# Attention q and k projected with the weights stationary and both token tiles as one moving operand, v of groups 0 to 2 first

## The chip, the cores and the metric

The kernel runs on one core of a Trainium2 chip. The metric is the device time of one execution in microseconds (us), as the median of several runs. TensorE (PE) multiplies matrices, VectorE (DVE) and ScalarE (ACT) do elementwise work and move results out of PSUM, GpSimd (POOL) and SyncE (SP) mostly start transfers.

## What is computed

Four layers on 256 tokens of width 1024, in fp32. Each layer is a SwiGLU block, a mixer and another SwiGLU block, each followed by a layer norm. The mixers of the four layers are a state-space mixer, "fox" attention, "moba" attention and the state-space mixer again. The change touches the two attention mixers.

```python
def fox_attention(x, w_in, b_f, w_out):           # 16 heads of 64
    q, k, v, f_logit = split(x @ w_in)            # 1024 + 1024 + 1024 + 16 columns
    cum = cumsum(log_sigmoid(f_logit + b_f))
    logits = q k^T * 64**-0.5 + (cum[q] - cum[k]), causal
    return softmax(logits) v  @ w_out

def moba_attention(x, w_in, w_out):               # one block of 256 keys for 256 tokens, so
    q, k, v = split(x @ w_in)                     # this is plain causal attention
    return softmax(causal(q k^T * 64**-0.5)) v @ w_out
```

## The kernel before

The 256 tokens are two tiles of 128. Each tile is a generator (`stream`, line 793), `sts[0]` and `sts[1]`, called tile 0 and tile 1 below (`t` in the code). The weights come in pieces of at most 128 x 2048 fp32 (1 MB). `load` (line 170) fetches a piece and splits it into `wh` (fp32r, by ACT) and the rest `wl` (by DVE). Activations are split likewise into `xh` and `xl` by `to_T` (line 204), after four PE transposes for each half. A product is three matmuls (`mm3`, line 186): `xh` with `wh`, `xh` with `wl`, `xl` with `wh`. The activations are the stationary operand and the weights move through, 512 columns a matmul in `proj512` and 256 in `proj256`.

The outer loop (lines 855 to 869) advances tile 0 by one piece and then tile 1 by the piece two behind, and lets tile 1 catch up at the end of a sublayer. There are five buffers for split pieces. The program order gives priorities. A planner places each engine's instructions by these priorities and by its own estimate of when operands are ready, so what is traced later may go ahead of what waits. `keep_in_program_order` puts an instruction behind everything traced before it on its engine. `tc.high_priority()` lifts layer norms and `to_T`.

An attention sublayer takes its pieces in the order of `ATT_ORDER` (line 44): V0 Q0 V1 Q1 V2 Q2 V3 Q3 and then the four pieces O of the output projection. There are four groups of four heads. Q of a group is two pieces, 256 columns of q and 256 of k side by side, and V is one piece (in fox V0 is two pieces of 1088 columns with the 16 gate columns). For each tile and group:

- `proj512` on the two Q pieces gives q and k with tokens on partitions, in one PSUM bank (24 matmuls of 512 columns).
- `stage_q` (line 672) copies them to SBUF (ACT, line 674), transposes them on PE in four blocks of 128 x 128 (line 199), and writes q times 0.125 (DVE, line 677) and k (ACT, line 678) with features on partitions.
- `stage_v` (line 722) copies v out of its bank. `stage_f` (line 640, fox, V0) first reads the gate columns of that bank.
- `stage_s` (line 682) makes the scores: the mask (line 690), in fox the bias rows (line 695), then q with k (line 702), for tile 1 in two blocks of 128 keys. The first of these is pinned by `keep_in_program_order`. Then comes the softmax.
- `att` (line 729) transposes the probabilities, multiplies them with v (line 747) and splits the result for `down` (line 248), the output projection.

PSUM has eight banks: `GA(0)` and `GA(1)` take the tags acc0 and acc1 with two banks each, shared with the accumulators of `down`; `T()` and `G()` have two each. `at(i, f, ...)` runs a stage behind piece i of its tile.

Of the kernel before, what the change touches and what calls it, by code (L numbers as in the profile page):

```python
# [7 lines left out]
F32 = mybir.dt.float32  # L8
# [7 lines left out]
D = 1024  # L16
# [22 lines left out]

SSM_ORDER = ["X0", "Z0", "X1", "Z1", "O0", "X2", "Z2", "X3", "O1", "Z3",
             "O2", "O3"]
ATT_ORDER = ["V0", "Q0", "V1", "Q1", "V2", "Q2", "V3", "Q3", "O0", "O1", "O2", "O3"]


def ssm_pieces():
# [30 lines left out]
def build(tc, x, wst, ln_g, ln_b, sm_rows, sm_conv, sm_nw, fx_b, out, plan=None):  # L78
# [26 lines left out]
    def tmp(cols, tag, bufs, dt=F32):  # L105
        return spool.tile([128, cols], dt, name=tag, tag=tag, bufs=bufs)

    ident = cpool.tile([128, 128], F32, name="ident")
    make_identity(nc, ident)
    mhalf = cpool.tile([128, 1], F32, name="mhalf")  # L110
# [91 lines left out]
        return tp  # L202

    def to_T(st, h):
        xh = spool.tile([128, KT, 128], FR, name=f"xh{st.t}", bufs=1)
        xl = spool.tile([128, KT, 128], FR, name=f"xl{st.t}", bufs=1)
        for half in range(2):
            tp = transposes(h[:, half * 512:half * 512 + 512], 4)
            sl = slice(half * 4, half * 4 + 4)
            for ins in split(tp.rearrange("p (a b) -> p a b", a=4), xh[:, sl], xl[:, sl]):  # L210
                if opening:
                    tc.keep_in_program_order(ins)
        st.xh, st.xl = xh, xl
# [51 lines left out]
    def proj256(st, ps, w):  # L265
        wh, wl = w
        for k in range(KT):
            mm3(ps[:, :256], st.xh[:, k], st.xl[:, k], wh[:, k * 256:(k + 1) * 256], wl[:, k * 256:(k + 1) * 256],
                k == 0, k == KT - 1)

    def act_split(src, n):
        tp = transposes(src, n)
# [139 lines left out]
    def ssm(st, j):  # L412
# [86 lines left out]
        def stage_back(g):  # L499
            cv = s.cv[g]  # L500
            h8 = slice(g * 8, g * 8 + 8)
            tp = T()
            for k in range(4):
                nc.tensor.transpose(tp[:, k * 128:(k + 1) * 128], cv[:, k, mine], ident)
            tp8 = tp.rearrange("p (a b) -> p a b", a=8)

            def times(tag, rows, bufs):
                o = tmp(512, tag, bufs)
                nc.vector.tensor_mul(o.rearrange("p (a b) -> p a b", a=8), tp8,
                                     rows[:, h8].unsqueeze(2).to_broadcast([128, 8, 64]))  # L510
                return o
            xds[g] = (times(f"xdt{t}", d.dt, 1 + t), times("xD", s.rows[:, 64:96], 2))
            if t == 0:
                s.xe[g] = times("xe", d.de, 1)
# [107 lines left out]
    def fox_small(j):  # L622
        if j in foxs:
            return foxs[j]
        consts()
        s = St()
        s.rows = tmp(16, "rows", 1)
        nc.sync.dma_start(s.rows, bc(fx_b[j:j + 1, :], 16))
        s.kT, s.v = {}, {}
        foxs[j] = s  # L630
        return s

    def attn(st, kind, j):
# [26 lines left out]
        else:  # L660
            key = ("m", j)
            if key not in foxs:
                consts()
                foxs[key] = St()
                foxs[key].kT, foxs[key].v = {}, {}
            s = foxs[key]
        ahs, ps_, vs, kv = {}, {}, {}, {}
        qT = spool.tile([128, 2, 128], F32, name="qT", tag="xD", bufs=2)

        bank = {}  # L670

        def stage_q(g):
            qk = tmp(512, "t2", 4)
            nc.scalar.activation(qk, bank.pop(g), AF.Copy)
            tp = transposes(qk, 4).rearrange("p (a b) -> p a b", a=4)
            kT = kv[g][:, 0:256].rearrange("p (a b) -> p a b", a=2)
            nc.vector.tensor_scalar_mul(qT, tp[:, 0:2], 0.125)
            nc.scalar.activation(kT, tp[:, 2:4], AF.Copy)
            if t == 0:
                s.kT[g] = kT  # L680

        def stage_s(g):

            kT = kv[g][:, 0:256].rearrange("p (a b) -> p a b", a=2)
            rs = spool.tile([128, 12], F32, name="rs", bufs=4)
            parts = [(kT, 0)] if t == 0 else [(s.kT[g], 0), (kT, 128)]
            nk = 128 * len(parts)
            Sv = [f()[:, :2 * nk].rearrange("p (h k) -> p h k", h=2) for f in (T, G)]
            for b in range(2):
                nc.tensor.matmul(Sv[b][:, :, nk - 128:nk], K["mlo"], rep4(2), start=True, stop=True,  # L690
# [6 lines left out]
                    if b == 0:  # L697
                        tc.keep_in_program_order(ins)
            for i in range(2):
                for kt, off in parts:  # L700
                    for b, half in enumerate(halves):
                        ins = nc.tensor.matmul(Sv[b][:, i, off:off + 128], qT[half, i], kt[half, i], start=False,
                                               stop=True, skip_group_check=True)
                        if (i, off, b) == (0, 0, 0):
                            tc.keep_in_program_order(ins)
# [14 lines left out]
            ps_[g] = pt  # L720

        def stage_v(g):
            kv[g] = tmp(512, "xe" if t == 0 and g % 2 else f"xdt{t}", 1 + t)
            vs[g] = kv[g][:, 256:512]
            nc.scalar.activation(vs[g], bank.pop(("v", g))[:, :256], AF.Copy)
            if t == 0:
                s.v[g] = vs[g]

        def att(g):

# [10 lines left out]
            blocks = [vs[g]] if t == 0 else [s.v[g], vs[g]]  # L741
            for i in range(2):
                for kb, v in enumerate(blocks):
                    for b in range(2):
# [22 lines left out]
            at(where["Q", 0, 1], stage_cum)  # L767
        for g in range(ATT_G):
            q = where["Q", g, 1]
            at(q, stage_q, g)  # L770
            wait = 2 if fox and g == 0 else 0
            at(q + 1 + wait, stage_s, g)
            at(where["V", g, int(fox and g == 0)], stage_v, g)
            at(q + 2 + wait, att, g)
        first_o = where["O", 0, 0]
        for i, (kind, g, n) in enumerate(pieces):
            if kind == "Q" and n == 0:
                ps = bank[g] = GA(0) if i < first_o else G()
            elif kind == "V" and n == 0:
                ps = bank["v", g] = GA(1) if i < first_o else G()  # L780
            w = yield
            if kind == "O":
# [1 line left out]
            elif kind == "V" and fox and g == 0:  # L784
                proj512(st, ps, n, w, 272)
            elif kind == "V":
                proj256(st, ps, w)
            else:
                proj512(st, ps, n, w)
            for f, a in post.get(i, ()):  # L790
                f(*a)

# [129 lines left out]
def pack_att(w_in, w_out):  # L922
    P = []
    dn = rows2(w_out)
    for it in ATT_ORDER:
        g = int(it[1])
        sl = slice(g * 256, g * 256 + 256)
        if it[0] == "Q":
            P += cols512(np.concatenate([w_in[:, 0:D][:, sl], w_in[:, D:2 * D][:, sl]], axis=1))
        elif it == "V0" and w_in.shape[1] > 3 * D:  # L930
            P += cols512(np.concatenate([w_in[:, 2 * D:3 * D][:, sl], w_in[:, 3 * D:]], axis=1))
        elif it[0] == "V":
# [60 lines left out]
```

## Time and profile before

| | |
|---|---|
| median of 3 runs | 2125.59 us (2124.63 to 2127.35) |
| the profiled execution | 2124.81 us, of it 2122.9 us span |
| PE / DVE / ACT / POOL busy | 99% / 69% / 55% / 23% of the span |
| granted TensorE clock, mean | 0.999 |
| fox attention | about 757 to 879 us |
| moba attention | about 1248 to 1372 us |

In the timelines a row is: start, duration, engine, line, operation, output and operands, shapes, count, and in brackets an idle time ahead of it and what ended it. Matmul durations include a modelled pipeline end, so two neighbours overlap; what a matmul costs in a stream is the distance between starts. "ga", "gu", "acc" and "tp" are PSUM banks, "t" the copy of q and k that `stage_q` transposes, "xe" and "xdt" the buffers of k and v.

### The profile page before, as it was taken

The numbers are of one execution on the slowest core, as the hardware profiler recorded it, in microseconds if no ns is written. First come the engines' busy times: TensorE is split into PE (matmuls) and PEld (weight loads), VectorE is DVE, ScalarE is ACT, GpSimd is POOL, SyncE is SP. The second block draws the span as 40 slices with busy tenths as digits, with TensorE's granted clock in tenths as the row PEclk, the third lists the DMA queues.
The fourth block names the chain that finished last, engine by engine and source line by source line (L and its number), as shares of the span: only waits on it lengthen the run. The fifth ranks groups of instructions, "written<-read, shape, count | busy, mean of one in ns | idle before, by whom it ended". The sixth has DMA issues, their size and how long they took to land.

```text
span 2122.9 us, 29645 instructions
## 1 busy us (share of the span) xinstructions
PE 2099.0 (99%) x10218; PEld 1735.6 (82%) x10218; DVE 1461.4 (69%) x2829; ACT 1177.0 (55%) x2453; POOL 480.9 (23%) x871
## 2 busy tenths in 40 slices
PE   8999999999999999999999999999999999999998
PEld 7888878888888888788888888788888888788886
DVE  6557888855765585766675575765575578888565
ACT  5545997544544455544444455544445449975442
POOL 2331000233143210043233300034223310002331
PEclk9999999999999999999999999999999999999999
DMA  9665654666576653476566653376666656446662
GB/s 316 224 229 203 215 171 172 217 232 224 189 256 227 224 201 122 165 235 230 204 245 230 222 193 139 123 247 238 225 221 232 221 205 220 173 161 221 230 227 95
DMA packets 227559, 441.72 MB, mean 208 GB/s; under 512 B 20752, under 2 KB 21072, under 8 KB 227408
## 3 DMA queue, kind: packets, MB, share of 16 engines
q1 hardware_dynamic: 198768, 397.73, 52.5%
q0 software_dynamic: 28640, 42.09, 6.8%
q8 instruction: 80, 1.31, 0.3%
q14 instruction: 71, 0.58, 0.1%
HBM read 417.61 MB, written 22.13 MB: 207 GB/s over the span
## 4 chain that ended last, share of the span: by engine, by line
PE 91%; DVE 4%; ACT 2%; DMA 1%; issue 1%; POOL 0%; SPq 0%; DVEq 0%; ACTq 0%
PE gu L187 16%; PE gu L190 16%; PE gu L191 16%; PE acc L191 9%; PE acc L187 9%; PE acc L190 9%; PE ga L187 3%; PE ga L190 3%; PE ga L191 3%; PE tp L199 3%; DVE wl L160 2%; PE gu L550 1%; DMA raw<-in_w_dram 1%; PE gu L747 1%; DVE cv L461 1%
## 5 line engine op out<-in xcount | busy, mean ns | idle before, releaser
L160 DVE TENSOR_TENSOR wl<-raw,wh 128x512 fp32r<-128x512 f32 (+1 forms) x1412 | 889.1, 680 | 363.1 <-ACT wh L159 361.7
L159 ACT ACTIVATE wh<-raw 128x512 fp32r<-128x512 f32 (+1 forms) x1412 | 778.8, 620 | 511.2 <-PE gu L191 230.0
L187 PE MATMUL gu<-wh,xh 128*128 128x512 f32 (+1 forms) x1600 | 619.4, 387 | 2.7 <-ACT wh L159 1.2
L190 PE MATMUL gu<-wl,xh 128*128 128x512 f32 (+1 forms) x1600 | 618.6, 387 | 0.0
L191 PE MATMUL gu<-wh,xl 128*128 128x512 f32 (+1 forms) x1600 | 618.1, 386 | 0.0
L291 POOL DMA_DIRECT2D aT<-turn x640 | 348.3, 551 | 488.4 <-issue 314.7
L187 PEld LDWEIGHTS gu<-wh,xh 128*128 128x128 f32 x1600 | 301.1, 188 | 65.0 <-ACT wh L159 2.0
L187 PE MATMUL acc<-wh,ah 128*128 128x512 f32 x896 | 352.7, 394 | 0.0
L191 PE MATMUL acc<-wh,al 128*128 128x512 f32 x896 | 351.9, 393 | 0.3 <-DVE al L160 0.3
L190 PE MATMUL acc<-wl,ah 128*128 128x512 f32 x896 | 351.5, 392 | 0.0
L190 PEld LDWEIGHTS gu<-wl,xh 128*128 128x128 f32 x1600 | 301.2, 188 | 60.5 <-DVE wl L160 1.0
L191 PEld LDWEIGHTS gu<-wh,xl 128*128 128x128 f32 x1600 | 301.2, 188 | 59.8 <-DVE xl L160 0.4
L315 ACT ACTIVATE t<-gu 128x256 f32<-128x256 f32 x176 | 67.5, 383 | 267.8 <-PE gu L191 247.2
L317 DVE TENSOR_TENSOR t<-t,gu 128x256 f32<-128x256 f32 x176 | 73.4, 417 | 189.6 <-ACT t L315 189.6
L191 PEld LDWEIGHTS acc<-wh,al 128*128 128x128 f32 x896 | 168.3, 188 | 36.5 <-DVE al L160 2.1
L187 PEld LDWEIGHTS acc<-wh,ah 128*128 128x128 f32 x896 | 168.3, 188 | 35.8 <-issue 1.3
L190 PEld LDWEIGHTS acc<-wl,ah 128*128 128x128 f32 x896 | 168.3, 188 | 34.5 <-issue 1.3
L287 POOL DMA_DIRECT2D turn<-tb x160 | 90.4, 565 | 330.9 <-DVE tb L285 298.5
L187 PE MATMUL ga<-wh,xh 128*128 128x512 f32 (+4 forms) x448 | 159.5, 357 | 0.4 <-ACT xh L159 0.4
L190 PE MATMUL ga<-wl,xh 128*128 128x512 f32 (+4 forms) x448 | 156.8, 351 | 0.0
L191 PE MATMUL ga<-wh,xl 128*128 128x512 f32 (+4 forms) x448 | 155.7, 349 | 0.0
L235 POOL TENSOR_TENSOR rstd<-ve,mhalf 128x1 f32<-128x1 f32 x24 | 22.7, 945 | 441.9 <-DVE ve L233 441.9
(181 smaller groups left out, 1655.5 us busy)
## 6 DMA issues: line engine op xcount, KB each, us to landing
raw<-in_w_dram SPq DMA_DIRECT2D x354, 1024.0 KB, 5.3
turn<-tb POOLq DMA_DIRECT2D x160, 128.0 KB, 3.1
aT<-turn POOLq DMA_DIRECT2D x640, 32.0 KB, 3.9
mt<-cums SPq DMA_DIRECT2D x32, 256.0 KB, 4.2
gb<-in_ln_g_dram SPq DMA_DIRECT2D x12, 512.0 KB, 4.7
gb<-in_ln_b_dram SPq DMA_DIRECT2D x12, 512.0 KB, 5.8
nw<-in_sm_nw_dram SPq DMA_DIRECT2D x8, 256.0 KB, 5.4
h<-in_x_dram SPq DMA_DIRECT2D x4, 256.0 KB, 4.9
```

Of the source, the lines that this page charges most:

```text
L159: a = nc.scalar.activation(wh, raw, AF.Copy)
L160: return a, nc.vector.tensor_sub(wl, raw, wh.bitcast(F32))
L187: first = nc.tensor.matmul(o, xh, wh, start=start, stop=False)
L190: nc.tensor.matmul(o, xh, wl, start=False, stop=False)
L191: nc.tensor.matmul(o, xl, wh, start=False, stop=stop)
L199: ins = nc.tensor.transpose(tp[:, j * 128:(j + 1) * 128], src[:, j * 128:(j + 1) * 128], ident)
L235: nc.gpsimd.tensor_tensor(rstd, ve, mhalf, op=ALU.pow)
L287: nc.gpsimd.dma_start(dr, b.rearrange("p q k t -> p (q k t)"))
L291: nc.gpsimd.dma_start(aT[32 * q:32 * q + 32].rearrange("p i k t -> p i (k t)"), dv[q])
L315: nc.scalar.activation(sg, gu[:, :256], AF.Silu)
L317: nc.vector.tensor_mul(a, sg, gu[:, 256:])
L461: nc.vector.scalar_tensor_tensor(cv[:, i], xb[:, i, k:k + S], w[:, k:k + 1], cv[:, i], op0=ALU.mult, op1=ALU.add)
```

## The change

The tiles' `xh` and `xl` become slices of one constant tile `x4`, laid out so that for each k-tile the columns are xh of tile 0, xh of tile 1, xl of tile 0, xl of tile 1. A Q piece now holds 256 columns of q or of k alone, over all eight k-tiles. Tile 0 does nothing with it. Tile 1 calls `proj_T`: for each half of 128 features and each k-tile, three matmuls with a 128 x 128 block of weights stationary and 256 columns (both token tiles) moving. The result has features on partitions already; `stage_q` copies it out once for both tiles, q by ACT with the factor, k by DVE, and no longer transposes. Scores of tile 1 take 256 keys in one matmul. V of groups 0 to 2 comes ahead of the first Q and V3 after the last. Buffers of v hold both tiles. The state-space mixer's "xe" buffer goes from one to two.

```diff
-ATT_ORDER = ["V0", "Q0", "V1", "Q1", "V2", "Q2", "V3", "Q3", "O0", "O1", "O2", "O3"]
+ATT_ORDER = ["V0", "V1", "V2", "Q0", "Q1", "Q2", "Q3", "V3", "O0", "O1", "O2", "O3"]
...
+    x4 = cpool.tile([128, KT, 4, 128], FR, name="x4")
...
-        xh = spool.tile([128, KT, 128], FR, name=f"xh{st.t}", bufs=1)
-        xl = spool.tile([128, KT, 128], FR, name=f"xl{st.t}", bufs=1)
+        xh, xl = x4[:, :, st.t], x4[:, :, 2 + st.t]
...
+    def proj_T(ps, w):
+        wh, wl = w
+        for f in range(2):
+            o = ps[:, f * S:f * S + S]
+            for k in range(KT):
+                sl = slice(k * 256 + f * 128, k * 256 + f * 128 + 128)
+                nc.tensor.matmul(o, wh[:, sl], x4[:, k, 0:2], start=k == 0, stop=False, skip_group_check=True)
+                nc.tensor.matmul(o, wh[:, sl], x4[:, k, 2:4], start=False, stop=False, skip_group_check=True)
+                nc.tensor.matmul(o, wl[:, sl], x4[:, k, 0:2], start=False, stop=k == KT - 1, skip_group_check=True)
...
-        def stage_q(g):
-            qk = tmp(512, "t2", 4)
-            nc.scalar.activation(qk, bank.pop(g), AF.Copy)
-            tp = transposes(qk, 4).rearrange("p (a b) -> p a b", a=4)
...
+        def stage_q(g, n):
+            o = tmp(512, "xdt1" if n else "xD", 2).rearrange("p (a b) -> p a b", a=2)
+            ps = bank.pop((g, n)).rearrange("p (a b) -> p a b", a=2)
+            if n:
+                nc.vector.tensor_copy(o, ps)
+                s.kT[g] = o
+            else:
+                nc.scalar.activation(o, ps, AF.Copy, scale=0.125)
+                s.qT[g] = o
...
-                for kt, off in parts:
-                    for b, half in enumerate(halves):
-                        ins = nc.tensor.matmul(Sv[b][:, i, off:off + 128], qT[half, i], kt[half, i], start=False,
...
+                for b, half in enumerate(halves):
+                    ins = nc.tensor.matmul(Sv[b][:, i], q[half, i], k[half, i], start=False, stop=True,
...
             if t == 0:
-                s.v[g] = vs[g]
+                s.v[g] = tmp(512, "xe", 2) if 0 < g < 3 else tmp(512, "xdt0", 1)
+            nc.scalar.activation(s.v[g][:, t * 256:t * 256 + 256], bank.pop(("v", g))[:, :256], AF.Copy)
...
-            at(q, stage_q, g)
-            wait = 2 if fox and g == 0 else 0
-            at(q + 1 + wait, stage_s, g)
+            if t == 1:
+                at(q - 1, stage_q, g, 0)
+                at(q, stage_q, g, 1)
+            at(q + 3 - t, stage_s, g)
             at(where["V", g, int(fox and g == 0)], stage_v, g)
-            at(q + 2 + wait, att, g)
+            at(q + 4 - t, att, g)
...
-            else:
-                proj512(st, ps, n, w)
+            elif t == 1:
+                bank[g, n] = GA(0)
+                proj_T(bank[g, n], w)
...
-            P += cols512(np.concatenate([w_in[:, 0:D][:, sl], w_in[:, D:2 * D][:, sl]], axis=1))
+            P += cols256(w_in[:, 0:D][:, sl]) + cols256(w_in[:, D:2 * D][:, sl])
```

## Rows read from the trace of the kernel before

**Rows 1.** The page: busy time and share of PE; clock in 40 slices.

```profile
PE 2099.0 (99%) x10218; PEld 1735.6 (82%) x10218; DVE 1461.4 (69%) x2829; ACT 1177.0 (55%) x2453; POOL 480.9 (23%) x871
...
PEclk9999999999999999999999999999999999999999
```

**Rows 2.** Busy time of each engine, clock and DMA, in fox and moba.

```profile
755.00:870.00 115.00, 114.15 (x744) 92.97 (x743) 76.78 (x168) 64.62 (x170) 7.37 (x13) 1.00 0.44 157
...
1260.00:1375.00 115.00, 114.74 (x736) 92.28 (x735) 71.98 (x134) 67.32 (x171) 0.92 (x1) 1.00 0.40 147
```

**Rows 3.** Timeline of PE: first and thirteenth of a run of 512-column matmuls.

```profile
741.85 0.39 PE L187 MATMUL gu<-wh,xh 128*128 128x512 f32 x1
...
744.57 0.39 PE L187 MATMUL acc<-wh,ah 128*128 128x512 f32 x1
```

**Rows 4.** Timeline of PE: 24 matmuls of 256 columns, first and what follows.

```profile
769.54 0.28 PE L187 MATMUL ga<-wh,xh 128*128 128x256 f32 x1
...
772.42 0.40 PE L187 MATMUL ga<-wh,xh 128*128 128x512 f32 x1
```

**Rows 5.** Timeline of PE: four transposes of q and k among 512-column matmuls.

```profile
836.20 0.39 PE L187 MATMUL ga<-wh,xh 128*128 128x512 f32 x1
836.43 0.60 PE L199 MATMUL tp<-ident,t 128*128 128x128 f32 x4
836.78 0.48 PE L190 MATMUL ga<-wl,xh 128*128 128x512 f32 x1
837.10 0.39 PE L191 MATMUL ga<-wh,xl 128*128 128x512 f32 x1
```

**Rows 6.** Timeline of PE: the same among 256-column matmuls.

```profile
839.31 0.28 PE L191 MATMUL ga<-wh,xl 128*128 128x256 f32 x1
839.56 0.66 PE L199 MATMUL tp<-ident,t 128*128 128x128 f32 x4
839.97 0.37 PE L187 MATMUL ga<-wh,xh 128*128 128x256 f32 x1
840.18 0.28 PE L190 MATMUL ga<-wl,xh 128*128 128x256 f32 x1
```

**Rows 7.** Timeline of PE: the same right behind scores, and with waits ahead.

```profile
779.01 0.66 PE L199 MATMUL tp<-ident,t 128*128 128x128 f32 x4 [0.17 <-DVE rowsT L373]
...
807.13 0.66 PE L199 MATMUL tp<-ident,t 128*128 128x128 f32 x4
807.54 0.48 PE L187 MATMUL ga<-wh,xh 128*128 128x512 f32 x1
...
811.51 0.66 PE L199 MATMUL tp<-ident,t 128*128 128x128 f32 x4 [0.25 <-ACT t L674]
...
1257.53 0.33 PE L199 MATMUL tp<-ident,t 128*128 128x128 f32 x1 [0.56 <-ACT t L674]
```

**Rows 8.** Timeline of PE: tile 1's scores and what follows; 512-column fp32 matmul.

```profile
842.86 0.27 PE L702 MATMUL tp<-xdt,qT 64*128 64x128 f32 x1
...
843.85 0.50 PE L187 MATMUL acc<-wh,ah 128*128 128x512 f32 x1
...
240.14 1.02 PE L527 MATMUL gu<-xe,t 128*128 128x512 f32 x2
241.00 1.67 PE L550 MATMUL gu<-xdt,mt 128*128 128x64 f32 x14
```

**Rows 9.** Timelines of PE, then of DVE: start of the fox sublayer.

```profile
756.85 0.28 PE L187 MATMUL ga<-wh,xh 128*128 128x272 f32 x1
...
762.60 0.39 PE L187 MATMUL ga<-wh,xh 128*128 128x512 f32 x1
...
764.34 0.39 PE L187 MATMUL ga<-wh,xh 128*128 128x272 f32 x1
...
765.66 0.16 DVE L642 TENSOR_TENSOR sm<-ga,rows 128x16 f32<-128x16 f32 x1
```

**Rows 10.** Groups by line: writes of both token tiles into one shared tile.

```profile
L482 DVE COPY xb<-tp 128x512 f32<-128x512 f32 (+1 forms) x16 | 10.4, 651 | 2.2 <-PE tp L199 2.2
```

More of the change, by code (lines that the diff above doesn't have):

```diff
@@ L513, in stage_back @@
             if t == 0:
-                s.xe[g] = times("xe", d.de, 1)
+                s.xe[g] = times("xe", d.de, 2)
             tp = T()
@@ L628, in fox_small @@
         nc.sync.dma_start(s.rows, bc(fx_b[j:j + 1, :], 16))
-        s.kT, s.v = {}, {}
+        s.qT, s.kT, s.v = {}, {}, {}
         foxs[j] = s
@@ L664, in attn @@
                 foxs[key] = St()
-                foxs[key].kT, foxs[key].v = {}, {}
+                foxs[key].qT, foxs[key].kT, foxs[key].v = {}, {}, {}
             s = foxs[key]
-        ahs, ps_, vs, kv = {}, {}, {}, {}
-        qT = spool.tile([128, 2, 128], F32, name="qT", tag="xD", bufs=2)
-        bank = {}
-        def stage_q(g):
-            qk = tmp(512, "t2", 4)
-            nc.scalar.activation(qk, bank.pop(g), AF.Copy)
-            tp = transposes(qk, 4).rearrange("p (a b) -> p a b", a=4)
[L676 to L680, printed above, removed]
+        ahs, ps_, bank = {}, {}, {}
+        def stage_q(g, n):
[7 more added lines that the diff above has]
+                s.qT[g] = o
         def stage_s(g):
-            kT = kv[g][:, 0:256].rearrange("p (a b) -> p a b", a=2)
+            nk = 128 * (1 + t)
+            q, k = s.qT[g][:, :, t * 128:t * 128 + 128], s.kT[g][:, :, 0:nk]
             rs = spool.tile([128, 12], F32, name="rs", bufs=4)
-            parts = [(kT, 0)] if t == 0 else [(s.kT[g], 0), (kT, 128)]
-            nk = 128 * len(parts)
             Sv = [f()[:, :2 * nk].rearrange("p (h k) -> p h k", h=2) for f in (T, G)]
@@ L699, in stage_s @@
             for i in range(2):
-                for kt, off in parts:
-                    for b, half in enumerate(halves):
-                        ins = nc.tensor.matmul(Sv[b][:, i, off:off + 128], qT[half, i], kt[half, i], start=False,
-                                               stop=True, skip_group_check=True)
-                        if (i, off, b) == (0, 0, 0):
-                            tc.keep_in_program_order(ins)
+                for b, half in enumerate(halves):
+                    ins = nc.tensor.matmul(Sv[b][:, i], q[half, i], k[half, i], start=False, stop=True,
+                                           skip_group_check=True)
+                    if (i, b) == (0, 0):
+                        tc.keep_in_program_order(ins)
             pt = [tmp(512, "mt", 5) for b in range(1 + t)]
@@ L722, in stage_v @@
         def stage_v(g):
-            kv[g] = tmp(512, "xe" if t == 0 and g % 2 else f"xdt{t}", 1 + t)
-            vs[g] = kv[g][:, 256:512]
-            nc.scalar.activation(vs[g], bank.pop(("v", g))[:, :256], AF.Copy)
             if t == 0:
-                s.v[g] = vs[g]
+                s.v[g] = tmp(512, "xe", 2) if 0 < g < 3 else tmp(512, "xdt0", 1)
+            nc.scalar.activation(s.v[g][:, t * 256:t * 256 + 256], bank.pop(("v", g))[:, :256], AF.Copy)
         def att(g):
@@ L740, in att @@
             o = G()
-            blocks = [vs[g]] if t == 0 else [s.v[g], vs[g]]
+            blocks = [s.v[g][:, n * 256:n * 256 + 256] for n in range(1 + t)]
             for i in range(2):
@@ L769, in attn @@
             q = where["Q", g, 1]
-            at(q, stage_q, g)
-            wait = 2 if fox and g == 0 else 0
-            at(q + 1 + wait, stage_s, g)
+            if t == 1:
+                at(q - 1, stage_q, g, 0)
+                at(q, stage_q, g, 1)
+            at(q + 3 - t, stage_s, g)
             at(where["V", g, int(fox and g == 0)], stage_v, g)
-            at(q + 2 + wait, att, g)
+            at(q + 4 - t, att, g)
         first_o = where["O", 0, 0]
         for i, (kind, g, n) in enumerate(pieces):
-            if kind == "Q" and n == 0:
-                ps = bank[g] = GA(0) if i < first_o else G()
-            elif kind == "V" and n == 0:
+            if kind == "V" and n == 0:
                 ps = bank["v", g] = GA(1) if i < first_o else G()
```

## The prediction

> **What bounds the kernel now.** I read the page first. PE is busy for 99% of the span, and the granted clock is at its upper level (2.4 GHz) in every slice [rows 1]. No other engine is near that. A page is an average, so I then looked at the two stretches that the change touches. In 115 us of fox PE is busy for 114.15, in 115 us of moba for 114.74, while DVE and ACT stand at two thirds or less and the DMA engines at 0.40 to 0.44 with about 150 GB/s [rows 2]. So in both places the order of work already fills PE, and the time changes by what PE must issue, not by what DVE, ACT or the transfers must do. PE's busy time has modelled ends, so I cost everything by distances between starts in the timeline.
>
> **What it costs PE to project in 256 columns.** Twelve matmuls of 512 columns take 744.57 - 741.85 = 2.72 us, or 0.2267 us each [rows 3]. Twenty-four of 256 columns take 772.42 - 769.54 = 2.88 us, or 0.1200 us each [rows 4]. Twice 0.1200 is 0.2400, so the same columns cost 13 ns more in two matmuls than in one. Before, q and k take 4 groups x 2 tiles x 24 = 192 matmuls of 512 columns in a layer, 384 in both layers. After, they take 4 groups x 2 pieces x 48 = 384 of 256 columns, 768 in both. 768 x 0.1200 - 384 x 0.2267 = 92.2 - 87.1 = **+5.1 us**, all of it on PE and so on the path. That the weights are now the stationary operand changes nothing I can see: the 256-column matmuls of before [rows 4] also load a 128 x 128 block each, and `x4[:, k, 0:2]` is 256 neighbouring columns, like their slices of `wh`.
>
> The Trainium skill ("TensorE: Matmul & The Clock Gate", section "Back-to-back issue gap") gives a gap of N/2.4 + 2.5 ns at full clock, which makes 109 ns for 256 columns and 216 for 512. By that the second matmul of a pair would cost 2.6 ns and not 13, and the change +1.0 us in place of +5.1, as an estimate. The trace has 120 and 227 ns, so I keep 5.1, and the rule gives the first rival below.
>
> **What it takes from PE.** `stage_q` ran 16 times (4 groups, 2 tiles, 2 layers), with four transposes each. Their price depends on what stands around them, so I looked at all 16.
>
> - Seven lie among 512-column matmuls, as in the first fence of this kind [rows 5]. From 836.20 to 837.10 is 0.90 us, where two matmuls alone take 0.45: 0.45 us each, 3.15 together. The matmul behind the transposes is late as well, which a count of transposes alone would miss.
> - Four lie among 256-column matmuls, as in the second [rows 6]. From 839.31 to 840.18 is 0.87 us, where two matmuls take 0.24: 0.63 us each, 2.5 together.
> - Two come right behind scores, where PE changes its kind of work anyway: 807.54 - 807.13 = 0.41 us each [rows 7], 0.8 together.
> - Three have a wait ahead, of 0.17, 0.25 and 0.56 us [rows 7]. With 0.45, 0.63 and 0.45 for the block itself that is 0.62, 0.88 and 1.01, 2.5 together.
>
> The sum is 3.15 + 2.5 + 0.8 + 2.5 = **-9.0 us**. As bounds, 16 x 0.41 = 6.6 us if every block were as cheap as the cheapest, 16 x 0.63 = 10.1 if as dear as the second kind.
>
> **Scores.** For tile 1 eight pairs of 128 columns become four pairs of 256 (each fp32 matmul has two records, and the two halves of 64 rows run side by side). Before, 842.86 to 843.85 is 0.99 us [rows 8]. A 512-column fp32 pass takes (241.00 - 240.14) / 2 = 0.43 us [rows 8], so 256 columns take about 0.215, and four of them with the same 0.1 us of change behind them 0.96. That is **0 us** within what I can read.
>
> **Edits at nothing.** The copies fall from 16 x (ACT 512 + DVE 256 + ACT 256) to 8 x (ACT 512 + DVE 512). ACT and DVE are under the bound [rows 2], so this gains nothing but slack; if that cover went, it would be a gain still. Weight bytes are unchanged. SP's queue has the same loads in the same places of the program, one for each piece and still two pieces ahead; a Q piece is now needed only when tile 1 comes to it, two pieces later. POOL's bias transfers keep their place behind Q0 and have two Q pieces (96 matmuls x 0.12 = 11.5 us) before tile 1's first scores read them. The second "xe" buffer only lets the state-space mixer write earlier.
>
> **New waits.** (a) In the first stretch of a sublayer tile 0 now has only V0, V1 and V2 to do before tile 1 is ready: since its Q pieces are empty. In fox V0 took 762.60 - 756.85 less the twelve matmuls of Q's first piece, 5.75 - 2.72 = 3.03 us [rows 3, 9]; with 48 x 0.120 for V1 and V2 that is 8.8 us. From tile 0's first matmul at 756.85 to tile 1's first at 764.34 is 7.5 us [rows 9], so the work just reaches. But V0, V1 and V2 of both tiles go through the two banks of acc1, where before V and Q had four. In fox the first bank is free only after `stage_f`'s read, which stood at 765.66 behind the layer norm on DVE [rows 9]; V2 would want a bank at 762.6, where Q's second piece started [rows 9]. The wait is at most 765.66 - 762.60 = 3.1 us, and nothing if V1's bank, which needs only an ACT copy, serves. PE also has tile 1's transposes to do there. I take 0.5 us, near the low end, and keep both. In moba there is no gate to read; I take 0, and 3.1 as the upper end. (b) The first score matmul of tile 0 is pinned behind `proj_T` of k and now waits for a DVE copy. Behind it queue tile 0's other scores, and PE has the next `proj_T` to put ahead. Nearest is the wait of 0.25 us on the copy [rows 7]: eight score blocks between 0 and 2.0 us together. Of 16 such handovers two waited for the copy [rows 7], so I take 0.4. (c) At the end tile 0's `att` of group 3 moves one piece later, behind O2, with tile 1's O0 (12 x 0.227 = 2.7 us) between it and tile 0's O3. Bounds are 0 and the 0.56 us of the longest such wait [rows 7] for each layer; I take 0. A gain on a wait below zero is excluded beyond what is counted, since little idle time is left [rows 2]: 0.85 + 0.26 us.
>
> **Sum.** +5.1 - 9.0 + 0.9 = -3.0 us. The profiled execution took 2124.81 us (span 2122.9 and 1.9 around it), which becomes 2121.8. It lies 0.8 below the median of the runs shown, 2125.59; against that median the forecast is **2122.6 us**, 0.14% less. Its own range goes from -5.9 (10.1 removed, 0.9 idle time gone, +5.1) to +1.0 (only 6.6 removed, 2.5 of waits), 2119.7 to 2126.6.
>
> **Rivals.**
>
> 1. *The second matmul is nearly free.* If a stationary weight block used twice in a row, as `wh` is in `proj_T`, let the pair run closer, the columns would run at the rate of the wide ones [rows 3], 0.2267 us for two matmuls, and the added 5.1 us would fall to 0. For it: two of every three loads bring the same block. Against it: `xh` stands twice in a row there too [rows 4], and the distances are even. Time 2125.6 - 9.0 + 0.9 = 2117.5 us. Chance 0.06. The formula of the Trainium skill quoted above points this way; the rows here do not agree with it.
> 2. *Tile 0 runs dry.* Wait (a) comes at its upper end in both layers, 2 x 3.1 = 6.2 us, with 0.4 of (b): 2125.6 + 5.1 - 9.0 + 6.6 = 2128.3 us, slower than before. It decides from 3.9 - 0.4 = 3.5 us of idle time over both starts, that is 1.75 us in each. For it: one engine's queue holds the bank in fox, and PE has no other stream there. Against it: V1's copy does not wait for DVE, Q0 can go ahead of V1 of tile 1 in its own bank, and moba has no gate. Chance 0.14.
> 3. *One tile, false waits.* `x4` joins four tiles. If a write of tile 1's slices waited for reads of tile 0's, or the other way round, every one of the 11 changes of sublayer would stand for the splits of `to_T`: ACT and DVE, twice each at about 0.65 us (651 ns for 512 columns [rows 10]), partly one after the other, so 2 to 3 us each, +22 to +33 us, about 2150 us. Against it: "xb" is also one tile with interleaved slices of both token tiles, and its copies wait for nothing but PE's transposes [rows 10]. Chance 0.04.
> 4. *The gain is not there*, because what followed the transposes was late anyway: 16 blocks at little, only the added 5.1 us seen, 2130.7 us. The timelines speak against it [rows 5, 6], with matmuls directly behind. Chance 0.02.
>
> **How the numbers follow.** The forecast has 0.74. About 0.2%, or 4.25 us, is what a measurement of this kernel can tell from no change, so faster begins at 2121.3. The forecast lies 1.3 us above that, and its range reaches 1.6 below: I give 0.26 of its 0.74 to faster and 0.48 to no change. With rival 1 faster is 0.32. Rival 2 is 2.7 us above the median, inside 0.2%, with a tail: 0.10 no change, 0.04 slower. Rivals 3 and 4 are slower, 0.06. So 0.32, 0.58 and 0.10. The range from 2117.5 to 2128.5 leaves out rivals 3 and 4, the tail of 2 and half of 1, some 0.13.
>
> **What would show it.** In the profile after: no "tp<-ident,t" transposes in either attention; 768 matmuls of 256 columns at 0.120 us on the lines of `proj_T`; PE as full as before in both stretches; each attention shorter by 1 to 2.5 us, and the other sublayers unchanged. Distances under 0.115 in `proj_T` would speak for rival 1, idle PE within 12 us of a sublayer's start and a first `proj_T` late for rival 2, idle PE at every change of sublayer for rival 3. I am wrong if the sublayers around move by more than 1 us, since then the planner's order elsewhere has changed, which I count at nothing.

## The result, and the profile after

The changed kernel takes **2149.97 us** (median of 5 runs, 2148.57 to 2152.47), beside 2125.59 for the kernel before in the same session. The ratio is 1.0113 (95% interval 1.0099 to 1.0128): 1.1% slower, where I had forecast 2122.6 us and a range up to 2128.5.

The page of the profiled execution of the changed kernel (span 2146.8 us):

```profile
PE 2124.7 (99%) x10474; PEld 1749.9 (82%) x10474; DVE 1460.7 (68%) x2821; ACT 1171.9 (55%) x2429; POOL 480.8 (22%) x871
...
PEclk9999999999999999999999999999999999999999
```

Beside [rows 1]: the clock is as full as before, and PE is still busy for 99%. The added 24 us are not idle time. PE's own busy time has grown by 25.7 us, with only 256 more records on PE.

To see where, I cut the span at the start of each sublayer (the first transposes of tile 0's input). First the kernel before, then the changed one: the SwiGLU block ahead of fox, fox, the SwiGLU block behind it, and moba. The columns are the stretch, its length, busy time and count of PE, PEld, DVE, ACT and POOL, the granted clock, the DMA share and GB/s.

```profile
572.20:752.71 180.51, 180.51 (x806) 149.01 (x805) 115.39 (x216) 85.03 (x175) 56.57 (x102) 1.00 0.65 227
752.71:877.69 124.98, 123.61 (x796) 99.93 (x796) 86.47 (x185) 71.30 (x185) 9.10 (x15) 1.00 0.43 153
877.69:1063.71 186.02, 186.02 (x832) 153.16 (x831) 119.12 (x223) 90.69 (x184) 56.58 (x102) 1.00 0.64 221
1245.84:1365.69 119.85, 118.67 (x765) 96.20 (x764) 77.55 (x143) 66.85 (x171) 1.84 (x2) 1.00 0.41 150
```

```profile
580.01:764.41 184.40, 184.40 (x807) 149.23 (x805) 115.44 (x216) 85.42 (x175) 56.55 (x102) 1.00 0.67 223
764.41:886.11 121.70, 120.31 (x925) 105.59 (x924) 85.37 (x181) 66.71 (x173) 9.11 (x15) 1.00 0.46 157
886.11:1075.96 189.85, 189.85 (x832) 153.30 (x831) 119.39 (x223) 91.18 (x184) 56.58 (x102) 1.00 0.65 216
1261.97:1377.63 115.66, 115.40 (x896) 102.37 (x894) 76.91 (x140) 62.41 (x159) 1.85 (x2) 1.00 0.47 156
```

Two things are to be seen. The attention layers did get shorter, fox by 3.3 us and moba by 4.2, more than the 3.0 together that I had forecast. And the SwiGLU blocks, which the change was not meant to touch, got 3.8 to 3.9 us longer, with the same number of matmuls and PE busy without a gap in both. Over the eight such blocks it is 2.7 to 3.9 us, in the two state-space mixers 1.0 and 1.2. So each matmul takes longer there. The timeline of PE in the changed kernel, where twelve matmuls on `ah` and `al` are followed by twelve on `x4` (the profile prints `x4` as "x"):

```profile
750.70 0.40 PE L190 MATMUL acc<-wh,ah 128*128 128x512 f32 x1
...
753.47 0.39 PE L190 MATMUL gu<-wh,x 128*128 128x512 f32 x1
...
756.27 0.40 PE L190 MATMUL acc<-wh,ah 128*128 128x512 f32 x1
...
790.28 0.28 PE L280 MATMUL ga<-x,wh 128*128 128x256 f32 x1
...
793.10 0.28 PE L280 MATMUL ga<-x,wh 128*128 128x256 f32 x1
```

Twelve of 512 columns with a block of `x4` stationary take 756.27 - 753.47 = 2.80 us, 0.2333 each, where the same twelve took 2.72, 0.2267 each [rows 3]. Over 4,745 neighbouring pairs of 512 columns whose second matmul has `x4` stationary the mean distance of starts is 233.5 ns; over 5,045 such pairs with `xh` or `xl` it was 227.3 (distances over 300 ns are left out). That is 4,745 x 6.2 ns = 29 us. The twelve on `ah`, a tile that did not change, take 2.77 us here: behind a stretch of `x4` the mean distances range over 226 to 236 ns and are back at 227 from the ninth on. Over 2,529 pairs the mean is 228.9 where the mended kernel below has 227.5, some 3 to 4 us more. In `proj_T`, where `x4` moves and the weights are stationary, 24 matmuls take 2.82 us, 0.1175 each, which is less than the 0.1200 that I had taken [rows 4].

### The profile page after: what moved, and what is told of

Same layout as the page of the kernel before. It is cut to its first block, busy times and chain, and to the rows that moved or that the text cites. A ratio compares the mean times of both kernels' runs of the same rounds, so it can differ in the third digit from the quotient of the medians.

```text
span 2146.8 us, 30132 instructions
## 1 busy us (share of the span) xinstructions
PE 2124.7 (99%) x10474; PEld 1749.9 (82%) x10474; DVE 1460.7 (68%) x2821; ACT 1171.9 (55%) x2429; POOL 480.8 (22%) x871
## 4 chain that ended last, share of the span: by engine, by line
PE 93%; DVE 3%; ACT 2%; DMA 1%; issue 1%; POOL 0%; DVEq 0%; ACTq 0%; SPq 0%
PE gu L193 17%; PE gu L190 17%; PE gu L194 17%; PE acc L190 9%; PE acc L193 9%; PE acc L194 9%; PE tp L202 2%; PE ga L190 2%; PE ga L194 2%; PE ga L193 2%; PE ga L280 1%; PE ga L282 1%; PE ga L281 1%; PE gu L563 1%; DMA raw<-in_w_dram 1%; DVE wl L163 1%
## 5 line engine op out<-in xcount | busy, mean ns | idle before, releaser
L193 PE MATMUL gu<-wl,x 128*128 128x512 f32 (+1 forms) x1600 | 631.8, 395 | 0.0
L190 PE MATMUL gu<-wh,x 128*128 128x512 f32 (+1 forms) x1600 | 627.7, 393 | 2.5 <-ACT wh L162 1.2
L194 PE MATMUL gu<-wh,x 128*128 128x512 f32 (+1 forms) x1600 | 623.5, 390 | 0.0
L190 PEld LDWEIGHTS gu<-wh,x 128*128 128x128 f32 x1600 | 301.1, 188 | 76.0 <-ACT wh L162 1.6
L194 PEld LDWEIGHTS gu<-wh,x 128*128 128x128 f32 x1600 | 301.2, 188 | 68.5 <-DVE x L163 0.4
L193 PEld LDWEIGHTS gu<-wl,x 128*128 128x128 f32 x1600 | 301.3, 188 | 67.3 <-DVE wl L163 0.5
L190 PE MATMUL ga<-wh,x 128*128 128x256 f32 (+4 forms) x320 | 107.1, 336 | 0.4 <-ACT xe L734 0.4
L194 PE MATMUL ga<-wh,x 128*128 128x256 f32 (+4 forms) x320 | 105.7, 332 | 0.4 <-DVE x L163 0.4
L193 PE MATMUL ga<-wl,x 128*128 128x256 f32 (+4 forms) x320 | 106.0, 332 | 0.0
```

The costliest lines, as they stand in the source:

```text
L190: first = nc.tensor.matmul(o, xh, wh, start=start, stop=False)
L193: nc.tensor.matmul(o, xh, wl, start=False, stop=False)
L194: nc.tensor.matmul(o, xl, wh, start=False, stop=stop)
```

## The experiments

Kernels of different sessions are compared by their ratios to the kernel before, which took 2126.98 us beside e1 to e4, 2124.45 beside e6 to e9 and 2125.88 beside e10 and e11.

**Theories.** What differs between an `xh` block before and an `xh` block in `x4`? (A) Where it begins, in bytes of its partition, as the built program allocates it. Before, xh0 began at byte 122,848 and wh at 8,160; both, and every k-tile of both, lie 480 bytes past a multiple of 512. In the changed kernel `x4` is the first constant, at 4,224, 128 bytes past, while the weights begin at 24,544 and the following multiples of 8,192, still 480 past. The stationary block then begins 160 bytes past the moving one, counted in a period of 256. (B) The layout, k-tiles 2,048 bytes apart with four slots interleaved. (C) One tile for both token tiles, at another place. (D) My third rival, false waits through that one tile. PE's unbroken busy time speaks against D already.

### The same layout with another begin (e1)

```diff
+    pad0 = cpool.tile([128, 88], F32, name="pad0")
+    nc.gpsimd.memset(pad0, 0.0)
     x4 = cpool.tile([128, KT, 4, 128], FR, name="x4")
+    pad1 = cpool.tile([128, 40], F32, name="pad1")
+    nc.gpsimd.memset(pad1, 0.0)
```

> The changed kernel, and nothing else, with x4 moved 352 bytes up (an unused tile of 352 bytes ahead of it, one of 160 bytes behind it), so that each of its 512-byte blocks begins at 480 within 512, as the separate xh and xl tiles of the kernel before did and as the weight tiles do in both kernels; as changed it begins at 128. Layout, waits and order of the instructions stay. Theory A (where a stationary block begins sets the distance of the matmuls that use it): 512-column matmuls on x4 go from 233.4 ns back to 227.3 ns; 4,870 x 6.1 ns = 29.7 us and some 3 us in the down projections, so about 2118 us, below both kernels. Theory B (the layout, with xh and xl interleaved and k-tiles 2,048 bytes apart) and theory C (one tile, written for both token tiles, low in memory): 233.4 ns and 2150 us as they are.

Measured: 2119.39 us, ratio to the kernel before 0.9967 (0.9955 to 0.9979). These 512 unused bytes, 352 of them ahead of `x4`, take 31 us off the changed kernel (1.0113 less 0.9967 is 1.46%). The windows of the four sublayers as above, and two runs of matmuls on `x4` (twelve of 512 columns, 24 of `proj_T`):

```profile
572.52:753.07 180.55, 180.55 (x807) 148.99 (x805) 115.43 (x216) 85.14 (x175) 56.56 (x102) 1.00 0.71 228
753.07:875.50 122.43, 121.16 (x924) 106.38 (x924) 85.33 (x181) 66.73 (x173) 9.11 (x15) 1.00 0.46 156
875.50:1061.43 185.93, 185.93 (x832) 153.12 (x831) 119.09 (x223) 90.90 (x184) 56.56 (x102) 1.00 0.68 220
1243.58:1359.89 116.31, 116.03 (x896) 102.97 (x894) 76.91 (x140) 62.46 (x159) 1.84 (x2) 1.00 0.46 155
```

```profile
742.20 0.39 PE L194 MATMUL gu<-wh,x 128*128 128x512 f32 x1
...
744.92 0.39 PE L194 MATMUL acc<-wh,ah 128*128 128x512 f32 x1
...
778.88 0.28 PE L284 MATMUL ga<-x,wh 128*128 128x256 f32 x1
...
781.76 0.28 PE L284 MATMUL ga<-x,wh 128*128 128x256 f32 x1
```

The SwiGLU blocks are back at 180.55 and 185.93 us, the twelve matmuls at 2.72 us, and the 24 of `proj_T` at 2.88, 0.1200 each. I call this version the mended kernel below. Run again beside e10 it took 2119.25 us, ratio 0.9969 (0.9957 to 0.9980):

> The mended changed kernel once more, for comparison on the same chip: 2119 us, 7 us less than the kernel before.

### The layout of the old tiles at the new begin (e2)

```diff
-    x4 = cpool.tile([128, KT, 4, 128], FR, name="x4")
+    x4 = cpool.tile([128, 4, KT, 128], FR, name="x4")
...
```

> The changed kernel with x4 as [128, 4, KT, 128] in place of [128, KT, 4, 128]: each of xh0, xh1, xl0, xl1 is 4,096 contiguous bytes, as the separate tiles of the kernel before were, in the same place (begins at 128 within 512). Theory B (layout): 227.3 ns, about 2118 us. Theories A (begin) and C (place, one tile): 233.4 ns, 2150 us; only the moving operand of the q and k projection is now two pieces 4,096 bytes apart, which may change its 117.7 ns.

Measured: 2150.65 us, ratio 1.0116 (1.0101 to 1.0131), 233.5 ns on `x4`. The layout has no part in it. B falls.

### Moving the weights instead (e3)

```diff
     x4 = cpool.tile([128, KT, 4, 128], FR, name="x4")
+    pad1 = cpool.tile([128, 40], F32, name="pad1")
+    nc.gpsimd.memset(pad1, 0.0)
```

> The changed kernel with 160 unused bytes behind x4: x4 stays at 128 within 512, and the weight tiles (wh, wl), ah, al and all tiles behind them move from 480 to 128 within 512. Theory A in its relative form (stationary and moving operand must begin alike): 227.3 ns on x4, and the down projections keep 227.4, about 2118 us. Theory A in its absolute form (a begin at 128 is slow for the stationary operand, 480 is fast): 233.4 ns on x4 and now about 233 ns on ah and al as well, 2,535 x 4 to 6 ns = 10 to 15 us more, 2160 to 2165 us. Theories B and C: 233.4 ns on x4, 227 to 229 on ah and al, 2150 us.

Measured: 2119.40 us, ratio 0.9968 (0.9955 to 0.9981); 227.1 ns on `x4`, 227.5 on `ah` and `al`. `x4` stands where it was slow, and is fast, since the weights now begin like it. So it is the difference of the two begins that counts, not either address.

### The kernel before with x4 (e4), and with its own tiles moved (e6)

```diff
+    x4 = cpool.tile([128, KT, 4, 128], FR, name="x4")
...
-        xh = spool.tile([128, KT, 128], FR, name=f"xh{st.t}", bufs=1)
-        xl = spool.tile([128, KT, 128], FR, name=f"xl{st.t}", bufs=1)
+        xh, xl = x4[:, :, st.t], x4[:, :, 2 + st.t]
```

> The kernel before with the x4 tile alone: to_T writes slots of x4 in place of xh0, xl0, xh1, xl1; the projections, the order of the attention pieces and all stages are those of before. Theories A, B and C alike: 512-column matmuls on x4 take 233.4 ns, which is 6.1 ns x about 5,100 = 31 us more, so 2157 us; the difference to the changed kernel's 2150 is what its attention layers gained, 7.5 us. Theory D (one tile joins four and adds waits, as my third rival had it): TensorE idles at the sublayer changes, its distances stay at 227 ns.

Measured: 2158.65 us, ratio 1.0155 (1.0138 to 1.0172), 233.5 ns over 5,046 pairs. e6 has no `x4` at all, only an unused tile of 160 bytes ahead of xh0 and one of 352 behind xl1:

```diff
+        if st.t == 0 and not opts:
+            pad0 = spool.tile([128, 40], F32, name="pad0", bufs=1)
+            nc.gpsimd.memset(pad0, 0.0)
...
+        if st.t == 1 and len(opts) == 1:
+            pad1 = spool.tile([128, 88], F32, name="pad1", bufs=1)
```

> The kernel before, and nothing else, with its four separate tiles xh0, xl0, xh1, xl1 moved up by 160 bytes (an unused tile of 160 bytes ahead of them, one of 352 behind), so that their blocks begin 160 bytes past those of the weight tiles, in a 256-byte period, as x4 does in the changed kernel. No x4, no change in attention. Theory A (difference of the begins): the 512-column matmuls on xh and xl go from 227.3 to 233.4 ns as on x4, 2158 us, as the kernel before with x4 had (2158.65). If one tile for all four slots, its layout or its place took any part: less than that, down to 2127.

Measured: 2158.22 us, ratio 1.0156 (1.0141 to 1.0171). The SwiGLU block ahead of fox, fox, and the block behind it:

```profile
580.03:764.43 184.40, 184.40 (x807) 149.14 (x805) 115.41 (x216) 85.43 (x175) 56.56 (x102) 1.00 0.63 223
764.43:890.72 126.29, 124.43 (x796) 100.06 (x795) 86.66 (x185) 71.39 (x185) 9.08 (x15) 1.00 0.43 151
890.72:1080.56 189.84, 189.84 (x833) 153.23 (x831) 119.18 (x223) 91.06 (x184) 56.57 (x102) 1.00 0.61 216
```

The untouched program, with four tiles moved by 160 bytes, loses 1.56%, as much as with `x4` (1.55%), and the blocks have the 184.40 and 189.84 us of the changed kernel. The difference of the begins is therefore enough by itself. C and D fall as well.

### The difference swept (e5)

For each pair of begins a small kernel, profiled in one execution at a granted clock of 1.00, has one group of 60 matmuls:

```diff
+    for s, m, n, kinds in SETS:
...
+        for r in range(20):
...
+            nc.tensor.matmul(o, xh, wh, start=r == 0, stop=False)
+            nc.tensor.matmul(o, xh, wl, start=False, stop=False)
+            nc.tensor.matmul(o, xl, wh, start=False, stop=r == 19)
```

> A small kernel of its own that computes nothing of the reference (it copies x to the output): on x as data, groups of 60 float32r matmuls of 128x128 stationary and n-column moving operand, back to back in the kernel's triples (xh with wh, xh with wl, xl with wh), one group for each pair of begins: the stationary block s bytes and the moving operand m bytes past the same point of a 512-byte period. What is read is the distance from start to start in each group, its first 20 matmuls left out. Theory A, relative form: 227 ns at 512 columns where s = m and about 233 ns where s - m is 160 or 352, whatever m is; s = m = 160 back to 227. Which other differences are slow isn't known: if the period is 64 bytes, all s that are multiples of 64 are at 227 and all odd multiples of 32 at 233; if it is 512, only s = 0. At 256 columns 120 ns where s = m and 117 to 118 ns at 160 and 352, as the q and k projections show in the runs so far. If the distances are the same at all s, the begin is not the cause by itself and something else of the full kernel takes part.

The first matmul of some groups in the timeline of PE. The name gives s, m and the columns n. Nothing lies between the groups, so each distance of two successive starts is 60 matmuls:

```profile
25.86 0.39 PE L116 MATMUL s0m0n512k<-mov,stat 128*128 128x512 f32 x1
39.47 0.39 PE L116 MATMUL s32m0n512k<-mov,stat 128*128 128x512 f32 x1
53.46 0.40 PE L116 MATMUL s64m0n512k<-mov,stat 128*128 128x512 f32 x1
...
95.44 0.39 PE L116 MATMUL s160m0n512k<-mov,stat 128*128 128x512 f32 x1
109.44 0.40 PE L116 MATMUL s192m0n512k<-mov,stat 128*128 128x512 f32 x1
123.19 0.40 PE L116 MATMUL s224m0n512k<-mov,stat 128*128 128x512 f32 x1
137.19 0.39 PE L116 MATMUL s256m0n512k<-mov,stat 128*128 128x512 f32 x1
150.79 0.39 PE L116 MATMUL s288m0n512k<-mov,stat 128*128 128x512 f32 x1
...
359.72 0.39 PE L116 MATMUL s160m160n512k<-mov,stat 128*128 128x512 f32 x1
373.34 0.39 PE L116 MATMUL s352m160n512k<-mov,stat 128*128 128x512 f32 x1
387.08 0.28 PE L116 MATMUL s0m0n256k<-mov,stat 128*128 128x256 f32 x1
394.27 0.28 PE L116 MATMUL s64m0n256k<-mov,stat 128*128 128x256 f32 x1
401.34 0.28 PE L116 MATMUL s128m0n256k<-mov,stat 128*128 128x256 f32 x1
```

With equal begins 60 matmuls take 13.61 us (25.86 to 39.47). At 32 they take 13.99, at 160 14.00, at 192 13.75, and at 256 13.60 again. At s = m = 160 they take 13.62: both operands at a begin where either alone is slow, and it is fast. Distances in ns, the first 20 matmuls of each group left out, by the difference s - m:

| difference in bytes | 0 | 32 | 64 | 96 | 128 | 160 | 192 | 224 | 256 |
|---|---|---|---|---|---|---|---|---|---|
| 512 columns | 226.7 | 233.4 | 233.4 | 234.2 | 232.2 | 233.3 | 228.9 | 233.3 | 226.7 |
| 256 columns | 120.0 | 118.4 | 117.8 | 118.6 | 118.6 | 120.1 | 117.8 | - | 120.1 |

The values from 288 to 480 repeat those from 32 to 224 within 0.1 ns: the period is 256 bytes. At differences of 4, 8 and 16 bytes the distances at 512 columns are 232.5, 230.7 and 233.3. Moving m by 32, 64, 160 or 352 instead of s gave what the same difference in the period gives (233.3, 228.9, 234.3 and 233.3). One stationary block for a whole group changed nothing (226.7 and 233.3). So the effect needs neither the kernel nor its other engines. It is not monotonic, and 256 columns are slightly faster at most unequal begins. There I had expected 117 to 118 ns at 160 and 352, and the sweep has 120.1 and 118.6.

### The sweep carried back (e7)

```diff
     x4 = cpool.tile([128, KT, 4, 128], FR, name="x4")
+    pad1 = cpool.tile([128, 56], F32, name="pad1")
+    nc.gpsimd.memset(pad1, 0.0)
```

> The changed kernel with 224 unused bytes behind x4, so that stationary blocks on x4 begin 192 bytes past the moving weight tiles in a 256-byte period (changed: 160; the mended kernel: 0). The sweep has 228.9 ns for this difference, 233.3 for 160 and 226.7 for 0. Theory A, with the sweep carried over: 2.2 ns x 4,750 = 10.5 us above the mended kernel's 2119.4, and about 1 us in the down projections that settle back, so 2130 to 2131 us. If only equal begins are fast in the full kernel: 2150 us. If 64 bytes of the difference are enough to be a multiple that is fast: 2119 us.

Measured: 2124.74 us, ratio 0.9998 (0.9989 to 1.0008). The distance is as the sweep says, 229.0 ns over 4,739 pairs; the time that I expected was 5 to 6 us too high. The windows of a SwiGLU block and of fox show most of it:

```profile
574.33:755.98 181.65, 181.64 (x806) 149.10 (x805) 115.47 (x216) 85.25 (x175) 56.58 (x102) 1.00 0.63 226
755.98:876.83 120.85, 119.13 (x924) 104.36 (x924) 85.35 (x181) 66.65 (x173) 9.11 (x15) 1.00 0.45 158
```

The block is 1.1 us above the mended kernel's, as it should be, but fox is 1.6 us below it, and so is moba: I had left out the matmuls of 256 columns, which gain at this difference.

### One term of my sum alone (e8)

```diff
-            tp = transposes(qk, 4).rearrange("p (a b) -> p a b", a=4)
+            tp = qk.rearrange("p (a b) -> p a b", a=4)
```

> The kernel before without the transposes of q and k in stage_q: qT and kT are written from the untransposed copy, so the scores are not those of the reference; the ACT copy, the DVE and ACT writes, all matmuls and all tiles stay. It measures one term of my sum alone. My sum: -9.0 us (bounds -6.6 and -10.1), so about 2117.5 us beside 2126.5 for the kernel before. The accounts of TensorE's distances in the two traces suggest less, since part of the delay around a transpose block could be a wait that stays: -5 to -7 us.

Measured: 2115.12 us beside 2124.45, ratio 0.9955 (0.9940 to 0.9970). Fox and moba:

```profile
751.88:872.71 120.83, 118.74 (x765) 96.38 (x764) 85.69 (x185) 71.67 (x185) 9.10 (x15) 1.00 0.44 158
...
1240.89:1354.86 113.97, 113.78 (x734) 93.06 (x732) 77.06 (x143) 67.20 (x171) 1.85 (x2) 1.00 0.44 158
```

Without the transposes the two layers lose 124.98 - 120.83 = 4.15 and 119.85 - 113.97 = 5.88, 10.0 us together; by the medians 9.3. The term of the sum was 9.0. The lower second guess of the expectation was wrong.

### v not ahead (e9)

```diff
-ATT_ORDER = ["V0", "V1", "V2", "Q0", "Q1", "Q2", "Q3", "V3", "O0", "O1", "O2", "O3"]
+ATT_ORDER = ["V0", "Q0", "V1", "Q1", "V2", "Q2", "Q3", "V3", "O0", "O1", "O2", "O3"]
```

> The mended changed kernel (x4 beginning like the weight tiles) with the pieces V0, Q0, V1, Q1, V2, Q2, Q3, V3 in place of V0, V1, V2, Q0, Q1, Q2, Q3, V3. It measures what bringing v ahead is worth. My prediction had 0.5 us of wait from the new order and up to 3.1; so without it the time should be the same or less than 2119.4 by up to 1 us. Rival: tile 0, which does nothing with a Q piece, has only V0 to do before tile 1 is ready, 3 to 4.5 us less work than it needs in each attention layer, so 3 to 9 us more, 2122 to 2128 us.

Measured: 2132.83 us, ratio 1.0037 (1.0024 to 1.0049), some 15 us above the mended kernel by the two ratios (13.5 by the medians), more than either theory said. Fox and moba in the windows, PE's waits in fox, and PE's longest wait in moba (for what, us in total, times, longest):

```profile
752.02:883.93 131.91, 124.30 (x925) 109.88 (x924) 86.26 (x181) 67.50 (x173) 9.10 (x15) 0.96 0.41 145
...
1252.02:1372.65 120.63, 117.75 (x896) 104.62 (x894) 77.48 (x140) 62.21 (x159) 1.84 (x2) 0.99 0.41 149
```

```profile
PE tp L709 <- DMA biases<-fbias: 4.0, 1, 4.0
PE tp L206 <- DVE h L249: 2.7, 1, 2.7
...
PE tp L206 <- DVE h L249: 2.5, 1, 2.5
```

Tile 0 does run dry: PE waits 2.7 us in fox and 2.5 in moba for tile 1's layer norm, and in fox 4.0 more for the bias transfers that the scores need. PE idles for 131.91 - 124.30 = 7.6 us in fox, and the granted clock of the stretch falls to 0.96; PE's busy time there is 3.1 us more than in the mended kernel for nearly the same count of records. Fox is 9.5 us longer than in the mended kernel and moba 4.3. The new order of v is what keeps this away.

### A begin for each use (e10)

The sweep wants equal begins for 512 columns and unequal ones for 256. On `x`, the SwiGLU blocks have only the first kind, and the attention layers only narrow matmuls. So `to_T` takes an offset. The layout of `x4` changes with it; e7 has the same differences in the attention layers with the old layout:

```diff
-    x4 = cpool.tile([128, KT, 4, 128], FR, name="x4")
...
+    x4 = cpool.tile([128, 4, KT * 128 + 64], FR, name="x4")
...
-                    to_T(st, st.h)
+                    to_T(st, st.h, 48 if kind == "mix" and mixer_of(l)[0] != "ssm" else 0)
```

> The mended changed kernel with a begin of its own for the attention layers: x4 as [128, 4, 1088] columns, of which to_T fills 1,024 from column 0 (begin equal to the weight tiles') ahead of SwiGLU and state-space sublayers, and 1,024 from column 48, 192 bytes further, ahead of the two attention layers, whose projections on x are all 256 columns wide (272 in one piece). The sweep has 226.7 ns for 512 columns at difference 0 and 117.8 ns in place of 120.0 for 256 columns at 192 (and at 64, which is what the q and k projection then has, with the operands exchanged). In the run at 192 everywhere the two attention layers were 120.85 and 114.68 us beside 122.43 and 116.31 in the mended kernel, 3.2 us less, and all other sublayers longer. Theory A: attention as at 192, the rest as mended, 2119.4 - 3.2 = 2116 us. If the interleaved writes at two begins make a tile wait for the other one's reads, PE idles at the six changes between attention and its neighbours: 2118 to 2125 us.

Measured: **2115.51 us**, ratio 0.9948 (0.9935 to 0.9960), beside 2119.25 for the mended kernel and 2125.88 for the kernel before in the same session. The four sublayers, and twice 24 matmuls of `proj_T`:

```profile
571.52:752.05 180.53, 180.53 (x807) 149.00 (x805) 115.40 (x216) 85.04 (x175) 56.54 (x102) 1.00 0.66 228
752.05:872.86 120.81, 119.10 (x923) 104.34 (x924) 85.30 (x181) 66.69 (x173) 9.12 (x15) 1.00 0.45 158
872.86:1058.82 185.96, 185.96 (x833) 153.10 (x831) 119.08 (x223) 90.81 (x184) 56.56 (x102) 1.00 0.64 221
1240.94:1355.43 114.49, 114.17 (x896) 101.08 (x894) 76.87 (x140) 62.46 (x159) 1.84 (x2) 1.00 0.44 157
```

```profile
783.82 0.28 PE L289 MATMUL ga<-x,wh 128*128 128x256 f32 x1
...
786.54 0.28 PE L289 MATMUL ga<-x,wh 128*128 128x256 f32 x1
...
797.61 0.28 PE L289 MATMUL ga<-x,wh 128*128 128x256 f32 x1
...
800.43 0.28 PE L289 MATMUL ga<-x,wh 128*128 128x256 f32 x1
```

The blocks are as in the mended kernel, the attention layers as in e7. `proj_T` runs at one of two distances here. Of the 721 within its stretches (under 130 ns), 434 lie at 113 to 115 ns, as in the first 24 (2.72 / 24 = 0.1133 us), below the sweep's 117.8 ns for this difference. The other 287 lie at 116 to 123, as in the second 24 (2.82 / 24 = 0.1175). The mean is 115.1 ns, where the mended kernel has 119.8 and the changed one 117.8. In e7, with the old layout, it is 368 and 353 of 721, so the layout does not bring the faster one about. What does is not settled.

## Why the prediction was wrong, point by point

**The step that failed** is a term put at nothing without a reason. "Edits at nothing" has no sentence on what it does to the SwiGLU and state-space sublayers that their stationary operand lies in another tile, and the forecast has "the other sublayers unchanged". I costed `x4` only in the part on projecting in 256 columns, where `proj_T` reads it, and there as "256 neighbouring columns". What the runs showed in its place is a price of +31 us: the mended kernel, where `x4` begins like the weights, is at 0.9967 of the kernel before and the changed one at 1.0113. The kernel before with `x4` alone (e4) loses 33 us (1.0155); it has 301 more pairs on `x4`, which at 6.2 ns are the 2 us between them. The mended kernel is 7 us below the kernel before, and 31 less 7 is the measured +24. No row of the kernel before shows the effect on 512 columns, since all its stationary and moving blocks of that width begin alike. What I could have read is where the tiles lie, and that a new first constant gives `x4` a begin of its own.

**Rival 3** had the time, about 2150 us, by luck, and named the new tile. Its mechanism was wrong: it wanted idle PE at every change of sublayer, and PE is busy without a gap (184.40 of 184.40 us). e6, which joins nothing, has the same loss. A rival that gives the right number is not thereby the cause; the row that it names has to be there.

**My own test worked, its reason did not.** I wrote that I am wrong if the sublayers around move by more than 1 us. They moved by 1.0 to 3.9. The reason that I gave, another order of the planner, is not it: the counts are the same (x806 and x807), and the mended kernel has the old lengths back.

**The terms for attention**, where the mended kernel is compared, so that only they are left:

- *Removed transposes, -9.0.* e8 has -10.0 by the windows and -9.3 by the medians. Right, within the bounds of 6.6 and 10.1.
- *Added columns, +5.1.* At equal begins `proj_T` runs at 0.1200 us, as taken (mean 0.1198). The size depends on the begins: at the means of 0.1178 in the changed kernel and 0.1151 in e10 the term is 768 x 0.1178 - 87.1 = 3.4 and 768 x 0.1151 - 87.1 = 1.3. Rival 1 asked for 0.1133, which e10 has in a good half of its distances. Its mechanism, a block used twice in a row, has no sign of its own here: one block for a whole group changed nothing (e5). The 2.6 ns that I estimated for the second matmul of a pair come to 2.5 by the same terms (218.3 - 215.8).
- *Waits, +0.9.* PE's idle time in the two layers was 1.37 + 1.18 = 2.55 us before and is 1.27 + 0.28 = 1.55 in the mended kernel: -1.0. I had excluded such a gain because only 0.85 + 0.26 us of idle time were left [rows 2]. Those windows begin at 755 and 1260 and so leave out the starts of the two layers; the wait of 0.56 us at 1257.53 [rows 7] lies outside the window from which I took the bound.
- *Together* -3.0 was forecast. The windows of the mended kernel give 2.55 + 3.54 = -6.1 in the attention layers. 1.9 of the 3.1 us missing are the waits, about 1.0 the transposes. In e8 PE's idle time in the two layers falls from 2.55 us to 2.28, so at most 0.3 of this is counted in both; the rest, 0.2 to 0.5 us, stays open.

**Rival 2**, tile 0 runs dry, did not happen: in fox of the changed kernel no wait of PE is over 0.4 us, the longest being

```profile
PE ga L194 <- DVE x L163: 0.4, 1, 0.4
```

The reckoning behind the rival (8.8 us of work for a gap of 7.5 us) holds; e9 takes V1 and V2 out of that gap and has the wait, 2.7 and 2.5 us.

**Rival 4** is refuted by e8.

## What to carry to other kernels

When a change gives an operand of TensorE a new tile, look where its blocks and those of the other operand begin, and keep the difference a multiple of 256 bytes for wide moving operands; a small constant allocated ahead is enough to shift it, and 160 unused bytes were worth 31 us here (e3). Where time is lost while the engine is busy without a gap and the counts are equal, compare the distance of starts of the same instruction in the two traces before looking for waits. And take the bound on idle time from windows that begin where the stage begins.

## What the runs showed of the hardware

The distance of back-to-back float32r matmuls (the type of `xh`, `xl`, `wh` and `wl`, fp32r above), each with a load of its own 128 x 128 block, depends on the difference of the begins of the stationary and the moving operand in their partitions, with a period of 256 bytes: 226.7 ns at 512 columns where it is 0, 229 to 234 elsewhere. At difference 0 the sweep has 226.7, 173.3 and 120.0 ns for 512, 384 and 256 columns at a granted clock of 1.00, the level of 2.4 GHz, which is 544, 416 and 288 cycles: 32 cycles, 13.3 ns, above one column a cycle at each of the three widths. The Trainium skill ("TensorE: Matmul & The Clock Gate", section "Back-to-back issue gap"), which I had weighed against the trace, has 2.5 ns there, in a formula that it gives for an isolated matmul; the closest of the float32r streams read here is `proj_T` in e7 and e10 at its faster distance, with 113.3 - 106.7 = 6.6 ns. Why the begins matter inside the chip is not shown by anything here. Nor is whose moving operand counts, the matmul's own or that of the one ahead of it, since within a stream all of them begin alike: in the changed kernel the mean distance from a matmul on `ah` or `al` to the first on `x4` is 236.0 ns (96 pairs; before, with `xh` or `xl`, 227.3), from one on `x4` to the first on `ah` or `al` 229.2 (105 pairs; before 226.9). Nor is why `ah` matmuls behind a stretch of `x4` need some nine matmuls to come back to 0.227 us.
